# A softmax unit's place for p is taken ahead of its exponential, and its high part is queued together with it

## The chip, the cores and the metric

The kernel runs on 1 core of one Trainium2 chip. The metric is the device time of one execution in microseconds. Engines are called by what they do in the profile: PE (TensorE matmuls), PEld (its weight loads), DVE (VectorE), ACT (ScalarE), POOL (GpSimd) and SP (SyncE, which issues nearly all DMAs).

## What is computed

One layer of a bidirectional encoder over a sample of 2048 tokens and a prompt of 512 tokens, width 1024. After an RMS norm, one projection gives all parts. Branch A is attention over a neighbourhood of 8 rows by 16 columns of a grid that is 64 columns wide, with 8 heads of 64 and a relative bias. Branch B is attention in a sliding window at three dilations (1, 4, 16), 8 heads each, whose three results are merged by the softmax of their log-sum-exps. Both branches are gated, projected, weighed with sigmoids and summed, and an output projection is added to the input. Cut to the core:

```python
h = rms_norm(x, norm_gain)
proj = einsum('bld,de->ble', h, w_in)                      # 1024 -> 9216
q_a, k_a = rms_norm(q), rms_norm(k)                         # branch A
o_a = softmax(q_a k_a / 8 + bias, window mask) v
for (win, dil) in ((128, 1), (512, 4), (2048, 16)):         # branch B
    q, k = rope(rms_norm(q)), rope(rms_norm(k))
    o, lse = softmax over keys t + m*dil, |m*dil| <= win/2
o_b = sum over groups of softmax(lse) * o
br_a, br_b = (o_a * silu(g_a)) w_branch_a, (o_b * silu(g_b)) w_branch_b
y = x + (sigmoid(m_a) * br_a + sigmoid(m_b) * br_b) w_out
```

## The kernel before

The stages follow one another on PE: dilated sweeps (`dil_sweeps`, dilations 1, 4, 16), neighbourhood sweeps (`na_sweeps`, two halves of four heads, each over sample and prompt), gate sweeps and an output sweep. PE's work is a sequence of tiles of 128 tokens (later blocks of 256), each multiplied with a bank of weights in two half-precision parts (high and low), three matmuls for each product. Attention is worked off beside it in small units.

A **unit** (`dil_block` and `na_group` make them, `softmax` runs them) is one to four heads of one block of queries; its scores fill 128 or 64 partitions by 512 or 384 columns. Its steps are: the score matmuls into an s tile of PSUM (two places); `top`, on VectorE, adds the mask and takes the maximum for each head, with the result in an e tile (`NE` = 2 places), and `neg` makes the bias of the exponential from the maximum on ScalarE or VectorE; `exp`, one ACTIVATE for each head on ScalarE, in place in e, with the sum of the row; `high`, the rounding of e to half precision into the first half of a p tile (`NP` = 4 places); `low`, the rest e - high into the second half, on VectorE or GpSimd, after which the e tile is free; `turn`, a transposing DMA on the SP queue from p into a pT tile (6 places), after which the p tile is free; and the matmuls with v (`pump`).

**What sets the order.** The kernel writes the whole program in one go, under a planner with a clock for each engine (`Clock`). Every step is a function that is put on a heap with a planned time; when PE's planned time passes it, the step emits its instructions at the end of their engines' queues and adds their planned cost to those engines' clocks. `clk.done` is the planned end of the last one plus a lag (`LAG_A` = 0.6 us for ScalarE, 0.35 for VectorE, 0.2 for GpSimd), and `clk.then(f)` plans f at that time. `Slots.take(f)` plans f when a place of a pool is planned to be free, and `Slots.give` frees one. `clk.first(A=..., V=...)` takes the engine whose queue is planned to end first with the cost given. The planned cost of a step doesn't know of its wait: an engine's clock runs on even where the instruction will have to wait for another engine. On the chip each engine then works through its queue in order, and semaphores see to the dependencies.

Costs that the planner uses here: a copy of N columns on ScalarE 0.155 + N/1200 us, on VectorE (`copy`) 0.15 + N/1920 + `PORT` (0.18); an exponential of n columns 0.155 + n/1200 + 0.135 + 0.28; `low` on VectorE 0.15 + N/960 + 0.18, on GpSimd 0.23 + N/480.

In the profile all of VectorE's operations have line L369, ScalarE's L364, GpSimd's L381, matmuls L356, transposes by DMA L408 and other DMAs L399, since helpers record them. So a step is found by its tiles: `e<-s,bm` or `e<-s,cmask` is `top`, `neg<-mx,sc` or `neg<-osb,sc` the bias, `e<-e,neg,sc` the exponential, `p<-e` `high` (CAST on DVE, ACTIVATE on ACT), `p<-e,p` `low`, `pT<-p` `turn`, and `o<-vc,pT` or `o<-dv,pT` the matmuls with v.

Of the kernel before, what the change touches and what calls it, by code (L numbers as in the profile page):

```python
# [16 lines left out]
FP16 = mybir.dt.float16  # L17
# [89 lines left out]
PORT = 0.18  # L107
# [160 lines left out]
class Enc:  # L268
# [549 lines left out]
    def softmax(self, u):  # L818
        clk, S, m, n, nh = self.clk, self.S, u["m"], u["n"], len(u["hs"])
        N = n * nh  # L820
        inv, ninv = (u["sc"][:m, i:i + 1] for i in range(2))

        def top():
            e = u["e"] = self.new("e", [128, 512])
            i = S["e"].index(e)
            x = u["mx"]() if "mx" in u else self.T.tile([128, 4], F32, name=f"mx{i}", bufs=1)[:m, :nh]
            u["neg"] = self.T.tile([128, 4], F32, name=f"neg{i}", bufs=1)
            for j in range(nh):
                c = slice(n * j, n * j + n)
                self.vec("tensor_tensor_reduce", e[:m, c], in0=u["s"][:m, c], in1=u["mask"](j)[:m, :n], scale=1.0,  # L830
                         scalar=BIG, op0=ALU.add, op1=ALU.max, accum_out=x[:, j:j + 1])
            S["s"].give(u["s"])
            u["topped"]()
            if clk.first(A=0.3, V=0.26) == "A":
                self.act(u["neg"][:m, :nh], x, scale=ninv, bias=SHIFT)
            else:
                self.vec("tensor_scalar", u["neg"][:m, :nh], x, ninv, SHIFT, op0=ALU.mult, op1=ALU.add, n=100)
            clk.then(exp)

        def exp():  # L840
            e = u["e"]
            for j in range(nh):
                c = slice(n * j, n * j + n)
                self.act(e[:m, c], e[:m, c], AF.Exp, bias=u["neg"][:m, j:j + 1], scale=inv, accum_out=u["den"](j))
            clk.then(S["p"].take, high)

        def high():
            p = u["p"] = self.new("p", [128, 1024], FP16)
            self.copy(p[:m, :N], u["e"][:m, :N])
            clk.then(low)  # L850

        def low():
            p = u["p"]
            self.either("tensor_tensor", p[:m, N:2 * N], u["e"][:m, :N], p[:m, :N], op=ALU.subtract)
            S["e"].give(u["e"])
            clk.at(clk.done + M_T, S["pT"].take, turn)

        def turn():

            pT = u["pT"] = self.new("pT", [128, 8, 128], FP16)  # L860
            self.turn(pT[:, :N // 64, :m], u["p"][:m, :2 * N])
            S["p"].give(u["p"])
            clk.at(clk.done + M_PV, ready)

        def ready():
            u["ready"] = True
            self.pump()

        top()

    def pump(self):
# [1343 lines left out]
```

## Time and profile before

| | us |
|---|---|
| median of 3 runs | 2845.07 (2841.5 to 2846.61) |
| the profiled execution | 2850.0 |
| its span, first to last instruction | 2847.9 |
| busy: PE / DVE / ACT / POOL | 2653.4 / 1612.5 / 1365.8 / 1460.0 |

The profile is of one execution. Shares of busy time are means over stages with different limits; so the rows below are given by stage where that matters. A wait row names the instruction that waited and the one that let it go, the total in us, how many times, and the longest. A timeline row has the start in us, the duration, the engine, the line, the operation, its tiles out<-in, and in brackets how long the engine had been idle ahead of it and for whom.

### The profile page before, as it was taken

What the parts mean: (1) busy time and instruction counts of PE and PEld (TensorE: products, weight loads), DVE (VectorE), ACT (ScalarE), POOL (GpSimd) and SP (SyncE); (2) the same over time, 40 slices, a digit from 0 to 9 for tenths busy, and PEclk for the clock granted to TensorE, in tenths of its full rate; (3) what the DMA queues carried; (4) which work ended last, traced back from release to release, by engine and by line L of the source; (5) the groups of instructions that cost most, each with busy time, mean ns of one, the idle gap of its engine ahead of it and who ended that gap; (6) DMA issues with size and microseconds to landing.
All of it is one profiled execution on the core that took longest, in us unless ns stands there. A gap on an engine that the chain in (4) does not pass through costs nothing. (4 is left out here: it accounts for less than half of the span.)

```text
span 2847.9 us, 55994 instructions
## 1 busy us (share of the span) xinstructions
PE 2653.4 (93%) x20853; PEld 1751.4 (61%) x20853; DVE 1612.5 (57%) x3716; ACT 1365.8 (48%) x3574; POOL 1460.0 (51%) x1996
## 2 busy tenths in 40 slices
PE   5998999989999999999899967799999999999999
PEld 2444444444444444455455544688888888888887
DVE  6787676785655765446686777432264544453111
ACT  5667666666666665656665667321132211222110
POOL 4887778777778898857665764100011221231110
PEclk9999999999999999999999975799999999999999
DMA  7898896776675765578998898431253444453443
GB/s 220 211 202 184 195 192 120 147 137 114 114 128 111 158 115 118 102 205 188 201 226 189 184 196 168 95 82 50 67 163 98 130 131 126 123 189 103 149 144 111
DMA packets 806721, 419.21 MB, mean 147 GB/s; under 512 B 688704, under 2 KB 733056, under 8 KB 800048
## 3 DMA queue, kind: packets, MB, share of 16 engines
q1 hardware_dynamic: 806016, 414.86, 63.4%
q8 instruction: 163, 2.67, 0.4%
q0 software_dynamic: 432, 0.77, 0.2%
q14 instruction: 110, 0.90, 0.1%
HBM read 171.72 MB, written 79.13 MB: 88 GB/s over the span
## 5 line engine op out<-in xcount | busy, mean ns | idle before, releaser
L356 PEld LDWEIGHTS <-hb 128*128 128x128 f16 x6240 | 590.3, 99 | 665.8 <-issue 109.2
L356 PE MATMUL proj<-wt,hb 128*128 128x512 f16 (+2 forms) x3420 | 691.4, 355 | 28.4 <-ACT qk L364 14.3
L356 PE MATMUL proj<-wu,hb 128*128 128x512 f16 x2880 | 663.3, 383 | 34.0 <-ACT qk L364 23.7
L356 PEld LDWEIGHTS <-wt 128*128 128x128 f16 x4560 | 445.8, 98 | 66.7 <-DMA hb<-htd 7.6
L364 ACT ACTIVATE sg<-proj,wi 128x256 f32<-128x256 f32 x240 | 113.0, 473 | 618.2 <-PE proj L356 615.6
L364 ACT ACTIVATE e<-e,neg,sc 128x256 f32<-128x256 f32 (+4 forms) x688 | 393.0, 572 | 5.1 <-DVE neg L369 2.9
L356 PE MATMUL proj<-hb,wt 128*128 128x256 f16 x2760 | 313.8, 273 | 9.8 <-DMA hb<-htd 7.4
L356 PEld LDWEIGHTS <-pT 128*128 128x128 f16 (+1 forms) x4560 | 227.4, 102 | 140.6 <-DMA pT<-p 65.3
L369 DVE TENSOR_TENSOR p<-e,p 128x512 f16<-128x512 f32 (+2 forms) x283 | 249.7, 883 | 65.6 <-ACT p L364 61.9
L381 POOL TENSOR_TENSOR sq<-qk,gcs 128x256 f32<-128x256 f32 x240 | 195.3, 834 | 164.3 <-DVE q_ssq L369 160.2
L381 POOL TENSOR_TENSOR qk<-qk,sq 128x512 f32<-128x512 f32 (+1 forms) x140 | 182.3, 1302 | 188.9 <-DVE qk L369 129.5
L369 DVE SCALAR_TENSOR_TENSOR qk<-s,binv,sg 128x256 f32<-128x256 f32 x160 | 77.1, 483 | 316.4 <-PE s L356 314.0
L356 PE MATMUL proj<-hb,kT 128*128 128x256 f16 x1920 | 227.5, 275 | 2.8 <-DVE kT L369 2.8
L381 POOL TENSOR_TENSOR hb<-sg,hb 128x256 f16<-128x256 f32 x66 | 53.4, 810 | 324.2 <-ACT hb L364 324.2
L356 PE MATMUL s<-hb,wt 128*128 128x256 f16 x1800 | 209.7, 273 | 2.2 <-DVE qk L369 2.1
L356 PEld LDWEIGHTS <-kT 128*128 128x128 f16 x1920 | 188.6, 99 | 26.6 <-DVE kT L369 3.1
L369 DVE CUSTOM_DVE_ANT_0 e<-s,cmask 128x256 f32<-128x256 f32 (+2 forms) x528 | 153.6, 344 | 64.5 <-PE s L356 53.7
L381 POOL TENSOR_TENSOR qk<-qk,q_y 128x512 f32<-128x512 f32 x160 | 177.4, 1113 | 4.8
L369 DVE CAST p<-e 128x512 f16<-128x512 f32 (+2 forms) x173 | 113.1, 654 | 108.1 <-ACT e L364 98.2
L369 DVE TENSOR_REDUCE q_ssq<-sq 128x8 f32<-128x512 f32 x160 | 108.8, 680 | 111.3 <-ACT sq L364 111.0
L381 POOL TENSOR_TENSOR qk<-qk,gcs 128x512 f32<-128x512 f32 x120 | 163.6, 1363 | 9.4
L369 DVE TENSOR_TENSOR qs<-qk,qs 128x512 f16<-128x512 f32 (+1 forms) x137 | 119.5, 874 | 79.3 <-ACT qs L364 77.0
(189 smaller groups left out, 3749.5 us busy)
## 6 DMA issues: line engine op xcount, KB each, us to landing
hb<-htd SPq DMA_DIRECT2D x40, 1024.0 KB
wr<-in_w_in SPq DMA_DIRECT2D x132, 256.0 KB
obd<-osb SPq DMA_DIRECT2D x50, 264.0 KB
hd<-xs SPq DMA_DIRECT2D x20, 512.0 KB
htd<-hb SPq DMA_DIRECT2D x10, 1024.0 KB
mad<-qk SPq DMA_DIRECT2D x40, 256.0 KB
e<-obd SPq DMA_DIRECT2D x40, 256.0 KB
sq<-mad SPq DMA_DIRECT2D x40, 256.0 KB
```

Of the source, the lines that this page charges most:

```text
L356: self.nc.tensor.matmul(out, a, b, start=start, stop=stop, **kw)
L364: self.nc.scalar.activation(out, x, func, **kw)
L369: getattr(self.nc.vector, ins)(out, *a, **kw)
L381: getattr(self.nc.gpsimd, ins)(out, *a, **kw)
```

## The change

`top` no longer goes on to `exp`, but asks for a place of p and goes to `place`, which makes the p tile and calls `exp` at once. `exp` emits the exponentials and, in the same planned moment, the high part. The engine for the high part is still the one whose queue is planned to end first, but the exponentials are in ScalarE's queue by then, and VectorE is charged 0.75 in place of 0.33 us beside its columns. `low` follows at the planned end of the high part, as before. Neither the operations nor the number of places change.

```diff
--- before.py
+++ after.py
@@ -835,19 +835,22 @@
                 self.act(u["neg"][:m, :nh], x, scale=ninv, bias=SHIFT)
             else:
                 self.vec("tensor_scalar", u["neg"][:m, :nh], x, ninv, SHIFT, op0=ALU.mult, op1=ALU.add, n=100)
-            clk.then(exp)
+            clk.then(S["p"].take, place)
 
         def exp():
             e = u["e"]
             for j in range(nh):
                 c = slice(n * j, n * j + n)
                 self.act(e[:m, c], e[:m, c], AF.Exp, bias=u["neg"][:m, j:j + 1], scale=inv, accum_out=u["den"](j))
-            clk.then(S["p"].take, high)
-
-        def high():
-            p = u["p"] = self.new("p", [128, 1024], FP16)
-            self.copy(p[:m, :N], u["e"][:m, :N])
+            if clk.first(A=0.155 + N / 1200, V=0.75 + N / 1920) == "A":
+                self.act(u["p"][:m, :N], e[:m, :N])
+            else:
+                self.vec("tensor_copy", u["p"][:m, :N], e[:m, :N], n=N / 2, more=PORT)
             clk.then(low)
+
+        def place():
+            u["p"] = self.new("p", [128, 1024], FP16)
+            exp()
 
         def low():
             p = u["p"]
```

## Rows read from the trace of the kernel before

**Rows 1.** Stretch: us, busy PE, PEld, DVE, ACT, POOL (counts), clock, DMA share, GB/s.

```profile
71.00:1240.00 1169.00, 1099.78 (x8156) 541.95 (x8154) 769.93 (x1916) 760.37 (x2132) 933.98 (x1294) 0.99 0.73 147
1240.00:1640.00 400.00, 374.04 (x3079) 214.79 (x3077) 277.76 (x653) 252.56 (x664) 261.01 (x412) 0.99 0.92 202
1640.00:1851.00 211.00, 151.87 (x1459) 108.35 (x1458) 137.38 (x337) 123.06 (x303) 80.47 (x84) 0.71 0.72 153
1851.00:2848.00 997.00, 990.83 (x8012) 870.05 (x8009) 378.01 (x703) 189.94 (x401) 152.24 (x157) 1.00 0.40 119
```

**Rows 2.** What PE waited for, 71 to 1240 us (total us, times, longest).

```profile
PE proj L356 <- ACT qk L364: 40.5, 34, 3.2
PE proj L356 <- DVE wm L369: 7.3, 5, 1.9
PE proj L356 <- DVE dv L369: 6.3, 4, 3.4
...
PE s L356 <- DVE osb L369: 3.7, 6, 1.3
```

**Rows 3.** The same, 1282 to 1851 us, and 1240 to 1640 us.

```profile
PE o L356 <- DMA pT<-p: 45.6, 36, 3.6
...
PE o L356 <- DMA pT<-p: 16.1, 20, 2.1
```

**Rows 4.** The chain that ended last, end of the tail (start, us, what).

```profile
1790.96 3.45 DMA pT<-p
...
1794.61 4.27 DMA pT<-p
```

**Rows 5.** Instructions on tile p, 71 to 1250 us (ns), and idle before them.

```profile
L369 DVE CAST p<-e x141: 408/493/1492, 84.3 to 1241.6; 128x512 f16<-128x512 f32 x122, 64x512 f16<-64x512 f32 x19
L364 ACT ACTIVATE p<-e x51: 612/614/631, 91.3 to 1079.2; 128x512 f16<-128x512 f32 x46, 64x512 f16<-64x512 f32 x5
...
  ACT e L364: 93.9, 77
```

**Rows 6.** The same view, 1640 to 1800 us.

```profile
L408 SPq DMA_TRANSPOSE pT<-p x54: 1209/1242/4795, 1642.2 to 1795.9; - x54
L364 ACT ACTIVATE p<-e x48: 505/613/631, 1643.4 to 1793.8; 128x512 f16<-128x512 f32 x32, 128x384 f16<-128x384 f32 x16
```

**Rows 7.** ScalarE in the tail, in order of time.

```profile
1718.64 0.81 ACT L364 ACTIVATE e<-e,neg,sc 128x512 f32<-128x512 f32 x1
1719.36 0.19 ACT L364 ACTIVATION_READ_ACCUMULATOR e<-e,neg,sc 128x1 f32 x1
1719.77 0.29 ACT L364 ACTIVATE neg<-mx,sc 128x1 f32<-128x1 f32 x1 [0.23 <-DVE mx L369]
1719.97 0.61 ACT L364 ACTIVATE p<-e 128x512 f16<-128x512 f32 x1
...
1721.20 0.19 ACT L364 ACTIVATION_READ_ACCUMULATOR e<-e,neg,sc 128x1 f32 x1
1721.42 0.63 ACT L364 ACTIVATE p<-e 128x512 f16<-128x512 f32 x1
```

**Rows 8.** VectorE in the tail, two maxima that use the same e tile.

```profile
1717.58 0.69 DVE L369 CUSTOM_DVE_ANT_0 e<-s,bm 128x512 f32<-128x512 f32 x1
...
1721.76 0.69 DVE L369 CUSTOM_DVE_ANT_0 e<-s,bm 128x512 f32<-128x512 f32 x1 [0.17 <-DVE p L369]
```

**Rows 9.** ScalarE in the neighbourhood stage, in order of time.

```profile
1429.07 0.18 ACT L364 ACTIVATION_READ_ACCUMULATOR e<-e,neg,sc 128x1 f32 x1
...
1431.25 0.61 ACT L364 ACTIVATE p<-e 128x512 f16<-128x512 f32 x1
```

**Rows 10.** The SP queue in the neighbourhood stage, two transposes in turn.

```profile
1438.20 5.18 SPq L408 DMA_TRANSPOSE pT<-p  x2
```

**Rows 11.** Groups of instructions by shape (busy us, mean ns | idle before).

```profile
L364 ACT ACTIVATE e<-e,neg,sc 128x256 f32<-128x256 f32 x272 | 159.4, 587 | 0.9
...
L369 DVE CAST p<-e 128x512 f16<-128x512 f32 x144 | 98.7, 686 | 90.8 <-ACT e L364 82.4 <-DMA pT<-p 7.1 <-ACT v L364 0.7
```

## What the change will do to the time: the prediction

> **What bounds the kernel now.** I read the busy time by stage first [rows 1]. From 1851 us to the end TensorE is busy 991 of 997 us: nothing that the change touches can shorten that part, it can only start earlier. Before it lie three stages that all hold softmax units. In the dilated stage (71 to 1240) TensorE lacks 69 of 1169 us; in the neighbourhood stage (1240 to 1640) 26 of 400 us; in the tail of that stage (1640 to 1851), where the last units are worked off and the gate stage can't open, 59 of 211 us, and what it does there runs at a mean granted clock of 0.71. So the tail is the place where a quicker unit turns straight into time; elsewhere a quicker unit only helps where TensorE waits for it.
>
> Who TensorE waits for comes next. In the dilated stage it is above all ScalarE's copy of a projection out of PSUM (40.5 us); VectorE's own three waits make 17.3 us together [rows 2]. From 1282 to 1851 it is the transpose of p (45.6 us), but only 16.1 us of that fall before 1640 [rows 3]. The chain that ended last passes the end of the tail over one such transpose after another [rows 4].
>
> Then the units themselves. In the dilated stage 141 of 192 high parts are casts on VectorE and 51 are copies on ScalarE; VectorE sat 93.9 us idle ahead of casts until the exponential ended [rows 5]. In the tail ScalarE has nearly all, 48 copies to 54 transposes [rows 6].
>
> **What the change does to the program.** The operations of a unit stay (maximum, bias, one to four exponentials, high part, low part, transpose). What moves is the moment at which the planner emits the high part, and the engine it takes. Now it waits for the planned end of the exponentials, 0.6 us of planned lag on top, and then for a place of p. After the change the place is asked for when the bias is planned to be done, and exponentials and high part are emitted together. Three things follow.
>
> *Copies on ScalarE start right behind their exponentials.* In the tail one exponential's last instruction ended at 1719.55 (1719.36 + 0.19) but its copy began at 1719.97, because the bias of the other unit stood ahead of it and itself waited for its maximum; the next unit's copy began 0.03 us after its exponential (1721.39 to 1721.42) [rows 7]. So about 0.4 us is lost in every second unit. Two e tiles circulate, and an e tile is free only when the low part is done; one of the two was used again after 4.18 us (1717.58 to 1721.76) [rows 8]. 54 units start their transposes in 1640 to 1800 [rows 6]; 27 pairs by 0.33 us (between the 0.4 seen here and the smaller gaps of other pairs) is 9 us. Some pairs stand behind weight loads instead, or are limited by the score matmuls, so I take **-6 us**, with -9 and 0 as ends.
>
> *In the middle of the neighbourhood stage* the gap is wider: an exponential that ended at 1429.25 got its copy at 1431.25 [rows 9]. But behind the low part stands the SP queue: two transposes issued together took 5.18 us there [rows 10], and the DMA share of that stage is 0.92 [rows 1]. A p that is ready earlier mostly waits there instead. What can be had is the 16.1 us of TensorE's waits for p before 1640, and units that no longer slide into the tail. I take **-4 us**, ends -16 and 0. Its price is that a place of p is held longer: by the exponentials, 0.8 to 1.6 us. There are four places, and at one unit in about 2.9 us of the tail (54 in 160 us) four last for 12 us of holding. I put that at nothing, hidden as long as the transposes are not slower than now; if that cover goes, exponentials wait for a place, and e with them.
>
> *High parts that stay on VectorE are queued before their exponentials have run.* Those casts then hold VectorE, which works in order, until the exponential is done; queued behind them are the projections' sums of squares, the low parts of q, k and v, and the next units' maxima, for which in turn ScalarE's biases and TensorE's scores wait. How many will they be? The rule compares planned queue ends: ScalarE is charged its backlog, the exponentials just queued and 0.58 us; VectorE its backlog and 1.02 us (both for 512 columns). For two exponentials of 256 (planned 1.57 us) VectorE loses only if its backlog is 1.13 us over ScalarE's; for one of 512, 0.56 us. Right after the maxima of a pair VectorE has some backlog, and the first of a pair goes to ScalarE as soon as anything else stands in that queue; the second mostly has its partner's exponentials ahead of it on ScalarE. So by hand I expect fewer on ScalarE in the dilated stage than "mostly" says, and take the share between a quarter (as now) and all.
>
> The price has an end from rows: one exponential of 256 columns takes 0.587 us [rows 11], a unit has two of these or up to four shorter ones, so a cast queued early holds VectorE for at most some 1.5 us; by 141 that is 212 us, of which 94 us are already spent so [rows 5]: 118 us more. VectorE is busy 770 of 1169 us [rows 1]; its slack of 399 us would fall to 281, and the 57.8 us that TensorE waits for ScalarE and VectorE [rows 2] would grow in proportion (399/281), by 24 us. At the other end all casts go away and nothing is lost. Most of what a cast delays has slack now (VectorE's own three waits are 17.3 us), and the low part follows its high part sooner. I take **+3 us**, ends -5 and +24. If ScalarE does get most copies, it does not cost much: 90 copies of 0.61 us are 55 us in 1169, beside 760 busy, and they stand ahead of copies out of PSUM by at most one copy at a time.
>
> *The rest of the order.* Every place granted at another planned time reshuffles weights, transposes and tiles. The longest single waits of TensorE in [rows 2, 3], 3.2 to 3.6 us, stand for what one such accident is worth; I take 0, and two of them with a little as ends, -8 and +8.
>
> Sum: -6 - 4 + 3 = -7 us. The profiled execution took 2850.0 us (span 2847.9), the median of the runs is 2845.07, 4.9 less; 2850.0 - 7 = 2843.0, on the scale of the median **2838 us**, -0.25%. About 0.2% (5.7 us) is what a measurement of this kernel can tell from no change.
>
> **The rivals.**
>
> *VectorE stands in its queue (slower).* The place is the cast that is queued ahead of its exponential. It decides when the rule sends most dilated units to VectorE, as my hand count leans, and when the next unit's maximum comes to stand behind such a cast, so that exponential and maximum no longer overlap. Then +24 us in the dilated stage; in the tail every unit that loses the overlap costs about an exponential (0.81 us, [rows 7]), up to 44 us for 54 units, of which the planner's order (it mostly emits both maxima of a pair first) should spare most. For it: 93.9 us of such waits exist already. Against: ahead of 77 of the 141 casts VectorE was already idle when the exponential ended [rows 5], so in more than half of the units nothing ready stood between. Price +22: 2867 us.
>
> *Nothing to be seen (same).* The SP queue and the full DMA engines set the pace of the units, and what is won ahead of the transpose is lost in front of it; the tail keeps its length because the order of its score matmuls sets it. For it: [rows 3, 4, 10]. Against: in the tail the gap between exponential and copy is in the loop of the e tile. 2845 us.
>
> *The casts on VectorE and GpSimd's work are in each other's way (more gain).* A cast of 512 columns takes 0.686 us in the mean and 0.408 us at the least [rows 11, 5], so 144 of them carry about 40 us of standing still. If they go to ScalarE, VectorE loses 122 x 0.686 = 84 us of 770 in the dilated stage, its slack grows from 399 to 483, and 57.8 us of waits shrink by 10 us in place of the +3: 2825 us. The Trainium skill ("SBUF — State Buffer", section "SBUF: two separate sides") has this as a rule: VectorE in a mode with two ports and GpSimd take one shared pair of ports as an exclusive lock for a whole instruction, and ScalarE never waits for it. The spread from 0.408 to 1.492 us agrees. Against the rival: the ScalarE copy is longer than an undisturbed cast (0.61 against 0.41), and the rule may leave the casts where they are.
>
> *The change doesn't do what it says*: the share on ScalarE stays as now or falls. That is the condition of the first rival and has no price of its own.
>
> **How the numbers follow.** Chances: forecast 0.40, VectorE in its queue 0.28, nothing to be seen 0.20, casts and GpSimd 0.12. The forecast's own range is 2826 to 2846; three quarters of it lie over 0.2% below the time before. Faster: 0.30 + 0.12 = 0.42; same: 0.10 + 0.20 = 0.30; slower: 0.28. The range takes the gains nearly together (-9 - 16 - 8 = -33: 2812) and reaches above to +24 in the dilated stage, with a little of the tail and the order: 2871. Both signs hold much of the chance, so the likeliest is a weak one.
>
> **What would show it.** In the profile after: the gap between the last exponential and a copy on ScalarE near 0.05 us in the tail, and e tiles reused in under 4 us; the end of the last transpose of p before 1794 us if the gain is there, and the stretch behind it as long as now. VectorE's idle time ahead of p's casts until an exponential ends: well under 94 us if the copies went to ScalarE, clearly above it for the first rival, then together with longer waits of ScalarE's bias for maxima and of TensorE for PSUM copies. The counts of casts and copies tell which. The forecast is wrong if the dilated stage ends more than 6 us later, or if the tail keeps its length although the gap is gone.

## The result, and the profile after

The changed kernel took **2990.38 us** in the median (2990.22 to 2994.9), against 2845.07 before: a ratio of 1.0518, 95% interval 1.0494 to 1.0542. It is slower by 145 us where 7 us of gain were forecast, and it lies outside the range.

First the count of the two forms of the high part. The instructions on tile p over the whole span after (ns least/median/most, first and last start; behind the semicolon the shapes, where a group of over 200 instructions is counted by every second or third of them):

```profile
L369 DVE CAST p<-e x240: 346/427/1490, 84.5 to 1934.5; 128x512 f16<-128x512 f32 x92, 128x384 f16<-128x384 f32 x20, 64x512 f16<-64x512 f32 x8
L364 ACT ACTIVATE p<-e x96: 522/630/632, 142.3 to 1918.7; 128x512 f16<-128x512 f32 x63, 128x384 f16<-128x384 f32 x24, 64x512 f16<-64x512 f32 x9
```

The prediction quotes what the change was to do: high parts "mostly" on ScalarE. It does the opposite: 96 of 336 are there. VectorE's row of the group, before and after (busy us, mean ns, idle time ahead of it and for whom):

```profile
L369 DVE CAST p<-e 128x512 f16<-128x512 f32 (+2 forms) x173 | 113.1, 654 | 108.1 <-ACT e L364 98.2
...
L369 DVE CAST p<-e 128x512 f16<-128x512 f32 (+2 forms) x240 | 144.3, 602 | 392.8 <-ACT e L364 384.6
```

The casts themselves kept VectorE busy for 31 us more; what VectorE stood idle ahead of them for an exponential went from 98.2 to 384.6 us.

Then the place. Busy time by stage after, cut where TensorE has done nearly as many matmuls as at the cuts of [rows 1] (the first cut is about 3 us behind the last maximum of the dilated stage, the third 55 us behind the start of the last transpose of p):

```profile
71.00:1351.00 1280.00, 1132.87 (x8167) 550.67 (x8166) 737.80 (x1923) 756.59 (x2117) 940.53 (x1304) 0.96 0.66 134
1351.00:1780.00 429.00, 379.58 (x3067) 216.55 (x3065) 287.27 (x682) 244.89 (x645) 268.25 (x411) 0.96 0.88 193
1780.00:1992.00 212.00, 153.89 (x1462) 110.42 (x1461) 136.17 (x342) 103.99 (x262) 98.90 (x109) 0.76 0.64 143
1992.00:2988.00 996.00, 990.36 (x8007) 869.60 (x8004) 376.94 (x703) 189.83 (x401) 152.36 (x157) 1.00 0.40 119
```

The last stage is as long as it was. The dilated stage is 111 us longer: TensorE's idle time there went from 69 to 147 us (1280 - 1133), and nearly the same number of matmuls took 33 us more at a mean granted clock of 0.96 in place of 0.99. Both are means over two levels of TensorE's clock, 2.4 and 1.2 GHz: in this stage it stood at the lower one for 113 us in 22 stretches after, and for 34 us in 8 before. The end of each stage is sharper in the last maximum with the dilated mask (`cmask`) and the last transpose of p. Before:

```profile
L369 DVE CUSTOM_DVE_ANT_0 e<-s,cmask x528: 270/288/425, 79.8 to 1236.8; 128x256 f32<-128x256 f32 x80, 128x128 f32<-128x128 f32 x64, 64x128 f32<-64x128 f32 x32
...
L408 SPq DMA_TRANSPOSE pT<-p x336: 1193/1242/4795, 86.9 to 1795.9; - x168
```

After:

```profile
L369 DVE CUSTOM_DVE_ANT_0 e<-s,cmask x528: 270/288/425, 80.0 to 1348.1; 128x256 f32<-128x256 f32 x80, 128x128 f32<-128x128 f32 x64, 64x128 f32<-64x128 f32 x32
...
L408 SPq DMA_TRANSPOSE pT<-p x336: 1193/1244/5266, 88.1 to 1936.9; - x168
```

1348.1 - 1236.8 = 111 us in the dilated stage, and 588.8 - 559.1 = 30 us in the neighbourhood stage with its tail. What stands behind took 1051.4 us after and 1052.0 before.

What TensorE waited for in the dilated stage, 71 to 1351 us after:

```profile
PE proj L356 <- ACT qk L364: 53.6, 23, 5.4
PE o L356 <- DMA pT<-p: 30.7, 25, 3.1
PE proj L356 <- DVE dv L369: 15.6, 3, 6.9
PE s L356 <- DVE osb L369: 12.4, 16, 2.6
```

Against [rows 2] the copies out of PSUM cost 13 us more in fewer and longer waits, the copy for dv and the scores' wait for maxima 9 us more each; and the transposes of p, of which nearly all waits lay behind 1282 us [rows 3], now hold TensorE here too.

Who waits for whom, whole span, TensorE, ScalarE, VectorE (us in total, times, longest). Before:

```profile
PE o L356 <- DMA pT<-p: 46.4, 39, 3.6
PE proj L356 <- ACT qk L364: 40.9, 35, 3.2
...
PE s L356 <- DVE mx L369: 17.6, 26, 1.7
...
ACT neg L364 <- DVE osb L369: 177.3, 139, 5.4
ACT neg L364 <- DVE mx L369: 98.3, 95, 4.4
```

After:

```profile
PE s L356 <- DVE mx L369: 63.0, 55, 4.8
PE proj L356 <- ACT qk L364: 55.6, 27, 5.4
...
ACT neg L364 <- DVE osb L369: 244.6, 149, 8.4
ACT neg L364 <- DVE mx L369: 175.4, 107, 7.5
...
DVE p L369 <- ACT e L364: 384.6, 202, 7.2
```

ScalarE's biases wait 144 us longer for maxima on VectorE (`osb`, `mx`), while VectorE waits 286 us longer for exponentials on ScalarE. The two engines hold each other up. TensorE's scores in turn wait 45 us longer for maxima of the neighbourhood stage (`mx`, 17.6 to 63.0 us). How the waits run through the queues is to be seen in the dilated stage. VectorE after, in order of time (start, duration, what, idle time ahead of it):

```profile
401.91 0.43 DVE L369 CAST p<-e 128x512 f16<-128x512 f32 x1 [1.53 <-ACT e L364]
403.08 0.43 DVE L369 CAST p<-e 128x512 f16<-128x512 f32 x1 [0.74 <-ACT e L364]
...
404.25 0.42 DVE L369 CUSTOM_DVE_ANT_0 e<-s,cmask 128x256 f32<-128x256 f32 x1
...
408.67 0.43 DVE L369 CAST p<-e 128x512 f16<-128x512 f32 x1 [2.74 <-ACT e L364]
...
410.18 0.68 DVE L369 TENSOR_REDUCE q_ssq<-sq 128x8 f32<-128x512 f32 x1
...
426.72 0.43 DVE L369 CAST p<-e 128x512 f16<-128x512 f32 x1 [3.36 <-ACT e L364]
...
427.89 0.42 DVE L369 CUSTOM_DVE_ANT_0 e<-s,cmask 128x256 f32<-128x256 f32 x1
```

ScalarE in the same stretch:

```profile
405.12 0.29 ACT L364 ACTIVATE neg<-osb,sc 128x2 f32<-128x2 f32 x1 [1.56 <-DVE osb L369]
406.03 0.30 ACT L364 ACTIVATE neg<-osb,sc 128x2 f32<-128x2 f32 x1 [0.61 <-DVE osb L369]
406.23 0.58 ACT L364 ACTIVATE qk<-proj 128x512 f32<-128x512 f32 x1
406.84 0.63 ACT L364 ACTIVATE sq<-qk 128x512 f32<-128x512 f32 x1
407.38 0.58 ACT L364 ACTIVATE e<-e,neg,sc 128x256 f32<-128x256 f32 x1
...
428.70 0.30 ACT L364 ACTIVATE neg<-osb,sc 128x2 f32<-128x2 f32 x1 [2.01 <-DVE osb L369]
```

And TensorE:

```profile
402.80 0.83 PE L356 MATMUL s<-kT,dq 64*128 64x256 f16 x12
...
406.86 0.38 PE L356 MATMUL proj<-wu,hb 128*128 128x512 f16 x1 [2.48 <-ACT qk L364]
...
423.42 1.44 PE L356 MATMUL s<-kT,dq 64*128 64x256 f16 x11 [0.33 <-DVE osb L369]
```

Read it backwards. TensorE stood for 2.48 us for a copy out of PSUM (`qk<-proj`, 406.23). On ScalarE that copy stood behind two biases, which waited 1.56 and 0.61 us for their maxima. The maxima (from 404.25) stood on VectorE behind a low part and two casts, which had waited 1.53 and 0.74 us for exponentials of the pair before. Here that is the smaller part of the 2.48 us: the scores themselves were done only at 403.63 (402.80 + 0.83), so the queue ahead of the maxima cost some 0.6 us, and the rest is the pair's own maxima and biases, with the copy behind them. But then it goes round again: the next cast waited 2.74 us, because its exponentials stood behind those biases, that copy and a square; and the sum of squares `q_ssq`, whose input was ready at 407.47 (406.84 + 0.63), ran at 410.18. One round on, the cast holds the maxima outright: scores that were done at 424.86 (423.42 + 1.44) got their first maximum at 427.89, because VectorE stood for 3.36 us, to 426.72, for a cast's exponentials, and ran that cast and its low part first; and ScalarE's bias waited 2.01 us for that maximum.

### The profile page after: what moved, and what is told of

Its sections match the earlier page's. It is cut to its first block, busy times and chain, and to the rows that moved or that the text cites. A ratio compares the mean times of both kernels' runs of the same rounds, so it can differ in the third digit from the quotient of the medians.

```text
span 2988.4 us, 56000 instructions
## 1 busy us (share of the span) xinstructions
PE 2694.3 (90%) x20853; PEld 1763.7 (59%) x20853; DVE 1587.5 (53%) x3757; ACT 1335.0 (45%) x3500; POOL 1492.5 (50%) x2029
## 4 chain that ended last, share of the span: by engine, by line
PE 45%; DVE 11%; ACT 10%; POOL 7%; issue 5%; DMA 4%; SPq 1%; DVEq 0%; ACTq 0%; POOLq 0%
PE proj L356 37%; PE s L356 7%; ACT e L364 6%; DVE p L369 4%; POOL qk L381 3%; DVE e L369 3%; POOL sq L381 1%; DMA pT<-p 1%; PE o L356 1%; POOL q_t L381 1%; DVE wt L369 1%; ACT qk L364 1%; ACT p L364 1%; ACT qs L364 1%; ACT neg L364 1%
## 5 line engine op out<-in xcount | busy, mean ns | idle before, releaser
L356 PEld LDWEIGHTS <-hb 128*128 128x128 f16 x6240 | 599.2, 100 | 728.8 <-issue 162.6
L356 PE MATMUL proj<-wt,hb 128*128 128x512 f16 (+2 forms) x3420 | 709.1, 362 | 36.7 <-ACT qk L364 16.5
L356 PE MATMUL proj<-wu,hb 128*128 128x512 f16 x2880 | 679.6, 390 | 56.5 <-ACT qk L364 37.7
L369 DVE CAST p<-e 128x512 f16<-128x512 f32 (+2 forms) x240 | 144.3, 602 | 392.8 <-ACT e L364 384.6
L381 POOL TENSOR_TENSOR qk<-qk,sq 128x512 f32<-128x512 f32 (+1 forms) x140 | 177.3, 1266 | 189.5 <-DVE qk L369 130.1
L369 DVE TENSOR_TENSOR p<-e,p 128x512 f16<-128x512 f32 (+2 forms) x260 | 235.5, 927 | 19.4 <-ACT p L364 18.2
L364 ACT ACTIVATE qs<-qk 128x512 f16<-128x512 f32 (+1 forms) x200 | 105.7, 534 | 149.7 <-POOL qk L381 143.3
L356 PE MATMUL proj<-wv,hb 128*128 128x512 f16 x660 | 157.7, 383 | 7.4 <-DVE dv L369 6.0
```

The lines of the kernel that those rows point to most:

```text
L356: self.nc.tensor.matmul(out, a, b, start=start, stop=stop, **kw)
L364: self.nc.scalar.activation(out, x, func, **kw)
L369: getattr(self.nc.vector, ins)(out, *a, **kw)
L381: getattr(self.nc.gpsimd, ins)(out, *a, **kw)
```

## The experiments

What they were to tell apart: that the wait for the exponentials now stands in VectorE's queue (theory 1 of the expectations); that a place of p is held longer; that the low part and the next units come too early; that the share of the engines moved; that the order at large was reshuffled. Diffs are against the changed kernel's `exp` unless said otherwise. Each result is a median, beside runs of the kernel before on the same chip, with the ratio's 95% interval.

**The place ahead, and nothing else.** The high part is emitted at the planned end of the exponentials again.

```diff
-            if clk.first(A=0.155 + N / 1200, V=0.75 + N / 1920) == "A":
-                self.act(u["p"][:m, :N], e[:m, :N])
-            else:
-                self.vec("tensor_copy", u["p"][:m, :N], e[:m, :N], n=N / 2, more=PORT)
+            clk.then(high)
+
+        def high():
+            self.copy(u["p"][:m, :N], u["e"][:m, :N])
             clk.then(low)
```

> Only the first half of the change: the place of p is taken ahead of the exponential, but the high part is emitted as before, at the planned end of the exponentials, on the engine that copy() picks. Theory 1 (casts that VectorE has in its queue ahead of their exponentials hold it): back to 2830 to 2860 us, VectorE's idle time ahead of casts until an exponential ends back near 98 us (385 in the changed kernel). Rival 2 (a place of p that is held longer holds the units up): most of the 145 us stays, over 2920 us, and exponentials or maxima wait for transposes of p.

Measured: 2857.64 us, 1.0044 (1.0028 to 1.0059), with 98.0 us of VectorE's waits ahead of casts. Holding the place from before the exponential, with what it reshuffles, accounts for 14 of the 145 us.

**All high parts early, all on ScalarE.**

```diff
-            if clk.first(A=0.155 + N / 1200, V=0.75 + N / 1920) == "A":
-                self.act(u["p"][:m, :N], e[:m, :N])
-            else:
-                self.vec("tensor_copy", u["p"][:m, :N], e[:m, :N], n=N / 2, more=PORT)
+            self.act(u["p"][:m, :N], e[:m, :N])
```

> The change with the high part on ScalarE in every unit, straight behind the exponentials; no cast is left on VectorE. Theory 1: no loss, 2825 to 2860 us, by the terms of the prediction for the tail and the middle 2840 or a little under. Rival 3 (what costs is ScalarE and VectorE coupled more tightly in the emitted order, or ScalarE's copies out of PSUM standing behind copies of p): over 2880 us, with TensorE's wait for ScalarE's qk well over 45 us.

Measured: 2849.33 us, 1.0021 (1.001 to 1.0031); the last transpose began at 1797.7 against 1795.9. This goes further than the "mostly" of the change. Without casts on VectorE the loss is gone, but no gain is left in its place. ScalarE's copies of p waited longer for transposes that still read their place of p, 37.5 us in place of 11.4:

```profile
ACT p L364 <- DMA pT<-p: 37.5, 28, 3.8
```

And a stretch of its tail shows what came in place of the gap. ScalarE, the end of a pair of units and the next bias:

```profile
1722.16 0.19 ACT L364 ACTIVATION_READ_ACCUMULATOR e<-e,neg,sc 128x1 f32 x1
1722.37 0.63 ACT L364 ACTIVATE p<-e 128x512 f16<-128x512 f32 x1
1723.81 0.29 ACT L364 ACTIVATE neg<-mx,sc 128x1 f32<-128x1 f32 x1 [0.80 <-DVE mx L369]
```

TensorE and VectorE:

```profile
1727.72 1.44 PE L356 MATMUL s<-kT,qT 64*128 64x512 f16 x5 [1.48 <-DVE mx L369]
...
1726.97 0.69 DVE L369 CUSTOM_DVE_ANT_0 e<-s,bm 128x512 f32<-128x512 f32 x1
...
1728.89 0.69 DVE L369 CUSTOM_DVE_ANT_0 e<-s,bm 128x512 f32<-128x512 f32 x1 [0.62 <-PE s L356]
...
1731.27 0.69 DVE L369 CUSTOM_DVE_ANT_0 e<-s,bm 128x512 f32<-128x512 f32 x1
```

The copy follows its exponential within 0.02 us (1722.35 to 1722.37), as forecast. But then ScalarE waits 0.80 us for a maximum, the score matmuls wait 1.48 us for the maximum that frees their PSUM place, and the next maximum waits 0.62 us for those scores. A pair of maxima comes every 4.3 us (1726.97 to 1731.27), so an e tile is used again after as long as in [rows 8], 4.18. In this stretch the loop through the score place, the maximum and VectorE's own queue (the maximum at 1731.27 waited for nobody, but stood behind other work) is as long as the one that was shortened.

**The low part later.** As the change, but for casts on VectorE the low part is planned for the true end of exponentials and cast.

```diff
+            end = clk.done
             if clk.first(A=0.155 + N / 1200, V=0.75 + N / 1920) == "A":
                 self.act(u["p"][:m, :N], e[:m, :N])
+                clk.then(low)
             else:
                 self.vec("tensor_copy", u["p"][:m, :N], e[:m, :N], n=N / 2, more=PORT)
-            clk.then(low)
+                clk.done = max(clk.done, end + 0.15 + N / 1920 + PORT + LAG_V)
+                clk.then(low)
```

> The change, but where the cast goes to VectorE the low part (and with it the release of the e tile and the next unit) is planned for the true end of cast behind exponentials, and not for the end that the planner's VectorE clock gives. The cast stays queued ahead of its exponentials. Theory 1 (the cast itself holds VectorE): still over 2930 us and over 300 us of idle time ahead of casts. Rival 4 (the planner takes the cast as done before its exponentials and emits low parts and next maxima too early): at most 2890 us.

Measured: 2999.69 us, 1.0544 (1.0526 to 1.0561), with 228 casts and 408.1 us of waits ahead of them. The cause is not that what follows the cast is emitted too early.

**The same place and the same rule, the high part emitted late.** The engine is chosen when the exponentials are queued, as in the change, but the copy or cast is emitted at their planned end.

```diff
-            if clk.first(A=0.155 + N / 1200, V=0.75 + N / 1920) == "A":
+            by = clk.first(A=0.155 + N / 1200, V=0.75 + N / 1920)
+            clk.then(high, by)
+
+        def high(by):
+            e = u["e"]
+            if by == "A":
```

> The change with its place of p and its choice of engine, made at the same planned moment by the same rule, but the high part is emitted at the planned end of the exponentials as before the change. Theory 1 (the moment of emission costs, not the engine): under 2875 us although most high parts still are casts on VectorE. Rival 5 (more casts on VectorE, 240 in place of 173, cost): over 2920 us.

Measured: 2871.59 us, 1.0097 (1.0082 to 1.0112), with 219 casts on VectorE and 142.2 us of waits ahead of them. Nearly the change's share of casts (240), but queued late, costs 28 us and not 145: the moment of queueing is the larger part by far.

**The wait alone.** High parts all on ScalarE; where the rule says VectorE (266 units) an operation of one column that reads the end of e is queued on VectorE in the cast's place. What it writes goes nowhere. The diff is against the kernel with all high parts early on ScalarE.

```diff
+            by = clk.first(A=0.155 + N / 1200, V=0.75 + N / 1920)
             self.act(u["p"][:m, :N], e[:m, :N])
+            if by == "V":
+                hold = self.T.tile([128, 1], F32, name="hold", bufs=1)
+                self.nc.vector.tensor_copy(hold[:m], e[:m, N - 1:N])
```

> The wait by itself. As e2 (every high part on ScalarE, straight behind the exponentials), but where the rule of the change would take VectorE, VectorE gets a copy of one column of e in the cast's place, which the planner is not told of: no work to speak of, only the wait for the exponentials in VectorE's queue. Its result goes nowhere. Theory 1 (the wait in VectorE's queue is the cost): 2940 to 3010 us, most of the way from e2 (2849) to the changed kernel (2990). Rival 6 (the casts' own work, their planned clock, or what follows them costs): under 2880 us.

Measured: 2956.21 us, 1.0392 (1.0377 to 1.0408). Two of its wait rows:

```profile
DVE hold L849 <- ACT e L364: 426.3, 236, 6.0
...
ACT e L364 <- DVE neg L369: 45.3, 58, 3.9
```

The way back from VectorE to ScalarE is in part another one here than after the change: exponentials wait 45.3 us for biases that VectorE makes behind such holds (5.3 us in the kernel with all high parts early on ScalarE), and ScalarE's own biases wait 224.5 us for maxima there (196.1).

**The same operation, with a shorter wait.** It reads the bias, which is ready before the exponentials, in place of e; the diff is against the wait alone.

```diff
-                self.nc.vector.tensor_copy(hold[:m], e[:m, N - 1:N])
+                self.nc.vector.tensor_copy(hold[:m], u["neg"][:m, 0:1])
```

> As e5, but VectorE's one-column instruction reads the unit's bias in place of its e tile: it stands in the same place of VectorE's queue and waits for ScalarE only until the bias is done, not for the exponentials behind it. If the length of the wait sets the cost (theory 1): VectorE's idle time ahead of it falls from 426 us to under 200, and the time lies clearly under e5's 2956 us, at 2850 to 2900. If any instruction at that place of the queue costs, whatever it waits for: 2930 us or more.

Measured: 2851.93 us, 1.0028 (1.0015 to 1.004). The instructions and what they waited for:

```profile
L849 DVE COPY hold<-neg x266: 133/145/156, 81.2 to 1789.6; 128x1 f32<-128x1 f32 x121, 64x1 f32<-64x1 f32 x12
its engine sat idle before it (us, times) until:
  ACT neg L364: 11.1, 37
```

With the same 266 instructions of some 0.15 us at the same places the kernel loses 0.28% when they wait 11 us in all and 3.92% when they wait 426 us (without them it is 0.21%). The order of the operations is the same on all engines, instruction for instruction; what differs is what the one column is read from, and with it the waits. That settles theory 1: a wait that stands in VectorE's queue is enough for a loss of some 104 us (3.92 - 0.28 = 3.64%), without any cast.

**All casts early on VectorE.**

```diff
-            if clk.first(A=0.155 + N / 1200, V=0.75 + N / 1920) == "A":
-                self.act(u["p"][:m, :N], e[:m, :N])
-            else:
-                self.vec("tensor_copy", u["p"][:m, :N], e[:m, :N], n=N / 2, more=PORT)
+            self.vec("tensor_copy", u["p"][:m, :N], e[:m, :N], n=N / 2, more=PORT)
```

> The change with the high part on VectorE in every unit, queued ahead of its exponentials: 336 such casts in place of 240. Theory 1, with the cost in proportion to the casts (141 us for 240, measured from e2, which has none): 2849 + 336 x 0.59 = 3047 us, 3020 to 3090. If the cost came from units that are split between the engines, it would be under 2960 us.

Measured: 2950.12 us, 1.0369 (1.0354 to 1.0385): a miss. 336 early casts cost less than 240, and the time is the one named for the rival that units split between the engines cost; the next run asks for that.

```profile
DVE p L369 <- ACT e L364: 341.5, 273, 4.6
```

The price doesn't follow the count of casts: one wait is 1.25 us here (341.5/273) and 1.90 us after the change (384.6/202).

**The hold behind every unit.** As the wait alone (the diff is against it), for all 336 units.

```diff
-            if by == "V":
+            if True:
```

> Every unit of 336: high part as a copy on ScalarE right behind the exponentials (as in e2_all_act), and an operation of one column on VectorE that reads the last column of e, queued at the same moment, for every unit (e5_hold_only had it for 266). Nothing of the computation is left out; the extra column goes nowhere. It asks why the kernel with all casts early on VectorE took 2950 us, less than the changed kernel with 240 of them. Theory 1a: what lengthens each hold is ScalarE's own copies, which stand between the exponentials and so put the next exponentials later: then the holds are as long as in e5_hold_only or longer (1.8 us each, over 450 us in all), and the time is 2960 us or more. Theory 1b: what lengthens the time is that the engine changes from unit to unit, so that the order on both queues is uneven; then with the hold behind every unit the time comes to 2950 us or less and each hold to 1.3 us or less.

Measured: 2960.06 us, 1.04 (1.0385 to 1.0416).

```profile
DVE hold L849 <- ACT e L364: 435.6, 284, 6.0
```

One wait is 1.53 us, between what the two theories asked for, and the time is at 1a's bound. It is also within 4 us of the wait alone with 266 holds (2956.21), so a hold that comes in some units only is no dearer than one in all. With the copies on ScalarE the waits are longer (435.6 us in all here, 341.5 us with casts alone), as 1a has it, but the times are 10 us apart, not the 40 us by which the changed kernel is slower than the one with all casts early.

**The planner is told of the wait.**

```diff
+            end = clk.done
             if clk.first(A=0.155 + N / 1200, V=0.75 + N / 1920) == "A":
                 self.act(u["p"][:m, :N], e[:m, :N])
             else:
+                clk.free["V"] = max(clk.free["V"], end)
                 self.vec("tensor_copy", u["p"][:m, :N], e[:m, :N], n=N / 2, more=PORT)
```

> The changed kernel, with one line more: where the rule has chosen VectorE, VectorE's planned clock is set forward to the planned end of the exponentials plus the lag of 0.6 us before the cast is charged, so that the planner knows of the wait. The cast is still queued early. Theory 1 (the wait itself stands in the queue, whoever plans it): the first cast still holds VectorE, but the planner then sees VectorE as busy, gives following high parts, low parts and biases more often to the other engines, and spaces the casts; casts fall from 240 to about 170, waits ahead of them from 385 us to 150 to 250 us, and the time to 2870 to 2930 us. Rival (the planner's ignorance is no part of it, only the place in the queue counts): 2970 us or more with waits of 350 us or more. Rival (its ignorance is all of it): under 2860 us with waits under 120 us.

Measured: 2940.84 us, 1.0334 (1.0317 to 1.0351), with 166 casts.

```profile
DVE p L369 <- ACT e L364: 378.4, 157, 7.2
```

Casts fell as expected, but their waits stayed (378.4 against 384.6 us), as the first rival has it, longer ones for fewer casts, and the time lies between what theory 1 and what that rival asked for. Still 50 us of the loss are gone: what the planner books around a wait that it knows of, the smaller number of casts included, is worth a third of the loss. What is left, 95 us, lies near the price of the wait alone.

**Late, all on ScalarE.** The kernel before, with one word changed in `high`.

```diff
-            self.copy(p[:m, :N], u["e"][:m, :N])
+            self.act(p[:m, :N], u["e"][:m, :N])
```

> The kernel before with one edit: the high part is always copied on ScalarE, at the old moment and with the place of p taken at the old moment. It sets the engine apart from the moment. If ScalarE's greater load were a cost of its own: over 2860 us. By theory 1 nothing is lost beyond 0.5%: 2840 to 2860 us.

Measured: 2881.73 us, 1.013 (1.0115 to 1.0146), slower than theory 1 expected: at the old moment the greater load of ScalarE is a cost of its own, 37 us. TensorE's wait for copies out of PSUM over the whole span, with the 40.9 us of before beside it:

```profile
PE proj L356 <- ACT qk L364: 65.8, 48, 4.3
```

With every high part on ScalarE the change's early place is worth 32 us (2881.73 - 2849.33). So its idea holds on that engine; but the kernel before, which sends half of its high parts to VectorE, is no slower without it.

**Two versions that might have beaten the kernel before.** In the first, the dilated stage has the early copy on ScalarE and the neighbourhood stage is as before (this diff and the next against the kernel before).

```diff
-            clk.then(exp)
+            if u["sc"] is self.sc[1]:
+                clk.then(S["p"].take, place)
+            else:
+                clk.then(exp)
...
-            clk.then(S["p"].take, high)
+            if "p" in u:
+                self.act(u["p"][:m, :N], e[:m, :N])
+                clk.then(low)
+            else:
+                clk.then(S["p"].take, high)
```

> A version that might beat both: in the dilated stage as e2 (place of p ahead, high part on ScalarE straight behind the exponentials), in the neighbourhood stage as the kernel before. e2 ended its dilated stage 2.7 us earlier than the kernel before in the profiles and lost in the neighbourhood stage, where ScalarE waited 37.5 us for transposes of p (11.4 before). If these two are the causes: 2838 to 2845 us, at or a little under the time before. If the place that is taken ahead costs in the dilated stage too: 2848 us or more.

Measured: 2848.44 us, 1.0014 (1.0003 to 1.0026), at the bound that was named for a cost of the early place in the dilated stage too, and no clear difference from the 2849.33 us with the early copy in both stages, although ScalarE's waits for a place of p fell from 37.5 to 11.8 us. In the second, the copy goes behind the exponentials only where a place of p is free at that moment by the planner's clock.

```diff
-            clk.then(S["p"].take, high)
+            q = S["p"].free
+            if q and q[0][0] <= clk.now:
+                S["p"].granted.append(q.pop(0)[1])
+                p = u["p"] = self.new("p", [128, 1024], FP16)
+                self.act(p[:m, :N], e[:m, :N])
+                clk.then(low)
+            else:
+                clk.then(S["p"].take, high)
```

> A version that might beat the kernel before: the exponentials never wait for a place of p; where one is free at the moment at which the exponentials are emitted, it is taken and the high part goes to ScalarE straight behind them; where none is, the high part is emitted as before. No cast stands ahead of its exponentials. If the place taken ahead was what cost e2 its 0.2% (ScalarE's 37.5 us of waits for transposes of p): 2825 to 2843 us. If ScalarE's load is the limit: 2845 to 2855 us, as e2 and e8.

Measured: 2857.9 us, 1.004 (1.0026 to 1.0053), slower than both expectations. Neither is faster than the kernel before; nor is any other here.

## Why the prediction was wrong

**What bounds the kernel, and where.** Right: the stretch behind the tail kept its length (1051.4 us, 1052.0 before), and all of the loss lies in the stages with units.

**The share of the engines.** The hand count was right to doubt the "mostly", and did not doubt it enough: ScalarE had 40 high parts of 191 in the dilated stage, a fifth, where the prediction took between a quarter and all and [rows 5] had 51 of 192. In the tail it was not carried through: there the rule gave VectorE 30 high parts and ScalarE 16, where [rows 6] had 48 on ScalarE. The tail's term of -6 us assumed copies on ScalarE that the rule didn't leave there.

**The step that failed: the price of a cast queued early.** It was put at +3 us, with +24 us as its end; the dilated stage grew by 111 us. Two parts of that working fell.

*How long a cast holds VectorE.* The end was "at most some 1.5 us", the unit's own exponentials. In the dilated stage VectorE waited 2.1 us each (278.3 over 132), and up to 7.2 us. The row of the waits from 71 to 1351 us after:

```profile
DVE p L369 <- ACT e L364: 278.3, 132, 7.2
```

The hold begins when VectorE comes to the cast, not when the exponential begins, and takes in all that ScalarE still has to do ahead of it: in the timeline 2.74 us at 408.67 and 3.36 us at 426.72. So where 118 us of additional hold were the end, 184 us (278.3 - 93.9) came.

*What a hold does to TensorE.* The end spread the hold over VectorE's slack: TensorE's 57.8 us of waits in proportion to it, 24 us. That treats VectorE as a pool of time. Even with the 184 us that came, the same proportion gives 57.8 x 399/215 = 107 us, 50 us more, and TensorE's idle time rose by 78. The holds stand in an order, and ScalarE's order waits back: its biases wait for maxima behind the cast (244.6 us in place of 177.3), and its copies out of PSUM stand behind the biases. And at the lower granted clock the stage's matmuls took another 33 us of busy time, for which the sum had no term at all. Which waits brought the clock down was not measured.

**The tail.** The mechanism was right where the copy goes to ScalarE: the gap of [rows 7] is gone in the kernel with all copies on ScalarE. The term of -6 us measured some -1 there: the last 59 maxima of the stage (those that began from 1639 us on before) took 150.6 us (1642.0 to 1792.6) where they had taken 151.6 (1639.7 to 1791.3), and the last transpose came at 1797.7 us, not before 1794. The prediction had this as the rival "nothing to be seen", on the order of the score matmuls, and argued that the gap lies in the loop of the e tile. The loop of score place and maximum was as long in the stretch shown above; whether it sets the pace of the whole tail was not tested.

**The middle of the neighbourhood stage.** -4 us was forecast; the stage with its tail took 563.6 us (1797.7 - 1234.1) in the kernel with all copies on ScalarE and 559.1 us before. There ScalarE's copies did wait for places of p (37.5 us over the span, 11.4 before), which the prediction had put at nothing; the version that took these waits away in the neighbourhood stage was not clearly faster, so what they cost is open. The price put at nothing, that of holding a place, and the reshuffled order, put at 0 with 8 us to either side, came to 14 us together in the kernel where the place alone was taken ahead; the runs don't part the two.

**The rivals.** "VectorE stands in its queue" is what happened, with its condition (the share on ScalarE fell, from 27 to 21% in the dilated stage) and the signs named for it (idle time ahead of casts, longer waits of biases for maxima and of TensorE for copies out of PSUM). Its price of +22 us was about a seventh of what it cost; for the tail it had up to 44 us, and the last 59 maxima took 20 us more (172.0 in place of 151.6). "Casts and GpSimd in each other's way" fell as a gain: without a cast of p on VectorE the time is 2849.33 us, not 2825. That they are in each other's way the traces do show: after the change all 70 casts of 512 columns that took over 0.6 us began while a GpSimd instruction ran, and the 86 that began while none ran took 0.41 to 0.43 us. That agrees with the rule of the Trainium skill that stood beside this rival ("SBUF — State Buffer", section "SBUF: two separate sides"). But taking those casts away didn't move the end.

**What stays open.** The early wait by itself costs about 104 us, in a kernel where it is as long as after the change (426 us in all, 385 there), and a planner that knows of it takes about 50 of the changed kernel's 145 away; these overlap, and the runs don't part them further. Why 336 early casts cost 40 us less than 240 was not settled: with casts alone one wait is shorter (1.25 us in place of 1.90), but the hold behind every unit shows that their sum doesn't give the time.

## What to carry to other kernels

Before an instruction is queued earlier on an in-order engine, ask what it will wait for, and price the hold from the moment that the engine reaches it until the producer's whole backlog is worked off; then follow who waits for what stands behind it, and whether one of those feeds the producer. If it does, the price isn't a share of slack but a loop through two engines. In this kernel an instruction could be emitted ahead of its input without such a cost on the engine that produces the input, and not on another. And before a gap in one loop is counted as gain, look whether another loop has the same period.

## What was not expected of the hardware

A kernel with 266 instructions of some 0.15 us on VectorE, 40 us of work, was 3.92% slower than before when they waited for the exponential and 0.28% when they waited for the bias. And where TensorE stood idle for more of the stage, its work itself took longer: with 147 us of idle time 8167 matmuls of the dilated stage took 1132.87 us at a mean granted clock of 0.96, with 69 us 8156 took 1099.78 us at 0.99 [rows 1].
